# Running the first attention head by head, starting the modulation sums with the first fillers, and moving the final norm's sums into PSUM

## The chip, the cores and the metric

The kernel runs on one NeuronCore of a Trainium2 chip. TensorE (PE) multiplies matrices, VectorE (DVE), ScalarE (ACT) and GpSimd (POOL) work elementwise, and SyncE (SP) issues transfers between the device's memory and the on-chip buffers SBUF and PSUM. Each engine runs its own instructions in order; semaphores tie the engines together. The metric is the device time of one execution in microseconds (us).

## The reference

One decoder layer in float32, 512 rows of width 1024:

```
mod = silu(c) @ w_ada + b        # shift1, scale1, gate1, shift2, scale2, gate2
u   = x*(1+scale1) + shift1
q,k,v | q_down,kv_down,k_rope | g_sb,g_mla = split(u @ w_in)
A:  w[t,s] = sigmoid(z) * prod_{s<j<t}(1 - sigmoid(z_tj)),  z = q.k/8,  8 heads of width 64, s < t
B:  latent attention, softmax, 8 heads of width 96
mixed = sigmoid(g_sb)*(oA @ w_sb) + sigmoid(g_mla)*(oB @ w_mla)
x = LN1(alpha*x + gate1 * (mixed @ w_out))
u2 = x*(1+scale2) + shift2
moe: best of 4 groups, in it the best 2 of 8 experts; h = silu(u2 @ wg) * (u2 @ wu); h @ wd, weighted
x = LN2(alpha*x + gate2 * moe)
```

## The kernel before

The large projections are split products: each float32 weight becomes a rounded part `whi` (ACT, L320) and a remainder `wlo` (DVE, L321), and three matmuls per 128 rows of the contraction replace one (L330). One item of 128 output columns has 24 of them.

**Fillers.** Projection items stand in a queue `fq` (L262 to L296). `pull(n)` emits the next n steps of the queue on PE; before an item runs, its weights and those of the two items behind it are loaded and its own and the next one's are split. Loads go through the tag `raw`, a ring of two 1 MB buffers. A "mod" item is one of 16 pieces of the modulation vectors that are needed later (gate1, shift2, scale2, gate2): one 1 MB load `ra` into the same ring, and two DVE operations that add it into `macc` (L447, L449). In the kernel before the mod items stand behind the q/kv-down items (5) and the gate items (11), so they all run while the first attention runs.

**First attention** (stick-breaking, `attention_sb`, L567). For every pair of heads and every block of 128 queries it emits both heads' score matmuls (`z`, L584: head 0 in rows 0 to 63, head 1 in rows 64 to 127 of the array), both masks (L586), then the transposes `px` of the previous pair (L563), then 11.5 filler steps. Between z and px lie, per head, two sigmoids on ACT, a scan on DVE (L626) and a multiplication on POOL (L628). The second attention uses `attention` (L595): one head and block a step, with the transposes of the step before (`lag`) behind the fillers; its scores are at L773 and its masks at L774.

**Output projection.** `load_wo` (L858) loads one quarter of w_out (1 MB, `rwo`); `split_wo` (L866) multiplies the quarters of the second column half with gate1 (L875) and splits (ACT L876, DVE L877); `evac_o` (L884) multiplies by gate1, adds the residual and takes LN1's statistics. The four quarters are queued as fillers (L946), and the quarters of the second column half, (1,0) and (1,1), are loaded again later (L954, L960).

**Experts.** Twelve units of experts follow, the last two called q2 and q3 here (four experts each): gate and up products (L1352), silu times up (`sl`, ACT L1360, DVE L1361), transposes `phT` (L1367), copy `hT` (L1375), down products `py` (L1382), multiplication by gate2 (L1392), and an indirect store of the rows to the buffer `Ys` (POOL, L1398). PE, SP and POOL follow the order of the code here; DVE and ACT are ordered by the framework's cost model, except in the last unit. Ahead of the end stand: `norm_rows` (L1416), eight POOL loads of the four norm rows into `lraw`; `split_rows` (L1425), which splits them into `lrow` on DVE; `select_rows` (L1434), 26 POOL operations that build the matrices picking q3's rows for each token; `select_tr` (L1445), their transposes `pse`; `broadcast` (L1454), which spreads a norm row over 128 partitions with matmuls `pb`; and the diagonals `dg` (L1533) of the expert weights.

**Final norm** (L1646 to L1746). For each of four tiles of 128 tokens, `rs` is alpha times the LN1 output; `gts` are the two expert rows of a token, read back from `Ys`. Columns 0 to 511 (h = 0) are summed in SBUF on DVE: `base` adds the picked rows from PSUM, `add_y` adds the two expert rows (L1673). Columns 512 to 1023 (h = 1) are summed in PSUM by matmuls (L1662, L1670, L1703). Then `moments` (L1680), the scale and shift of a row (`scales`, L1686 and L1687), the normalisation on ACT (L1690), and gain and shift (L1694 and L1698) split between DVE and POOL. The overflow loop (L1602 to L1643) stands ahead of it: with these inputs its count is zero, and it is skipped.

## Time and profile before

| | us |
|---|---|
| median of 3 runs (lowest to highest) | 787.39 (787.24 to 788.0) |
| the profiled execution's own time | 790.91 |
| its span, first to last instruction | 789.2 |
| PE busy | 670.1 (85%) |
| DVE busy | 493.1 (62%) |
| mean granted TensorE clock | 0.937 |

The profiled execution is 3.5 us above the median, and its span is 1.7 us below its own time. All positions below are microseconds from the span's start. Up to 100 the projections of the first attention run, from 100 to 310 the first attention with its fillers, then the second attention, from 425 to 445 the output projection, from about 505 to 743 the experts, and from 743 on the last unit's second half and the final norm.

### The profile page before, as it was taken

The numbers are of one execution on the slowest core, as the hardware profiler recorded it, in microseconds if no ns is written. First come the engines' busy times: TensorE is split into PE (matmuls) and PEld (weight loads), VectorE is DVE, ScalarE is ACT, GpSimd is POOL, SyncE is SP. The second block draws the span as 40 slices with busy tenths as digits, with TensorE's granted clock in tenths as the row PEclk, the third lists the DMA queues.
The fourth block names the chain that finished last, engine by engine and source line by source line (L and its number), as shares of the span: only waits on it lengthen the run. The fifth ranks groups of instructions, "written<-read, shape, count | busy, mean of one in ns | idle before, by whom it ended". The sixth has DMA issues, their size and how long they took to land. (4 is left out here: it accounts for less than half of the span.)

```text
span 789.2 us, 10724 instructions
## 1 busy us (share of the span) xinstructions
PE 670.1 (85%) x3337; PEld 419.6 (53%) x3337; DVE 493.1 (62%) x1074; ACT 250.8 (32%) x545; POOL 176.5 (22%) x246
## 2 busy tenths in 40 slices
PE   5999998889989998899999873877699699972990
PEld 4778866656767775566788662433253233330230
DVE  3354379967775458977684686774725615741488
ACT  2133244533333435444341452712101110201411
POOL 2008024122233413200000013111101101136714
PEclk9999999989999999999999895989899989995996
DMA  9959763365652111361369478797999988999722
GB/s 281 344 141 336 232 220 116 114 207 180 236 179 80 44 30 34 127 184 54 107 226 365 157 279 287 254 388 252 410 407 409 382 334 314 344 405 346 307 116 106
DMA packets 83455, 184.15 MB, mean 233 GB/s; under 512 B 15442, under 2 KB 48815, under 8 KB 77499
## 3 DMA queue, kind: packets, MB, share of 16 engines
q1 hardware_dynamic: 76576, 171.70, 60.9%
q0 software_dynamic: 6736, 11.57, 4.2%
q8 instruction: 37, 0.61, 0.3%
q14 instruction: 32, 0.25, 0.1%
q10 hardware_dynamic: 74, 0.03, 0.0%
HBM read 173.30 MB, written 28.33 MB: 255 GB/s over the span
## 5 line engine op out<-in xcount | busy, mean ns | idle before, releaser
L1352 PE MATMUL pgu<-ex,xT 128*64 128x512 f32 (+1 forms) x608 | 115.0, 610 | 8.9 <-DMA ex<-in_w_exp_up_dram 5.7
L330 PE MATMUL acc<-uh,whi 128*128 128x512 f32 x224 | 91.5, 409 | 1.2 <-ACT whi L320 1.2
L330 PE MATMUL acc<-uh,wlo 128*128 128x512 f32 x224 | 89.7, 401 | 2.4 <-DVE wlo L321 2.4
L330 PE MATMUL acc<-ul,whi 128*128 128x512 f32 x224 | 89.2, 398 | 0.0
L1352 PEld LDWEIGHTS pgu<-ex,xT 128*64 128x64 f32 (+1 forms) x608 | 50.9, 129 | 66.8 <-issue 54.7
L1382 PE MATMUL py<-ex,hT 128*64 128x512 f32 (+1 forms) x304 | 63.9, 680 | 12.7 <-DVE hT L1375 8.0
L628 POOL TENSOR_TENSOR w<-be,sc 128x128 f32<-128x128 f32 (+3 forms) x32 | 41.7, 1314 | 120.2 <-DVE sc L626 62.7
L1360 ACT ACTIVATE sl<-pgu 128x256 f32<-128x256 f32 x33 | 11.5, 383 | 171.2 <-PE pgu L1352 136.7
L321 DVE TENSOR_TENSOR wlo<-raw,whi 128x1024 fp32r<-128x1024 f32 x27 | 38.8, 1445 | 21.7 <-ACT whi L320 21.7
L330 PEld LDWEIGHTS acc<-uh,wlo 128*128 128x128 f32 x224 | 42.9, 192 | 14.4 <-DVE wlo L321 3.4
L330 PEld LDWEIGHTS acc<-uh,whi 128*128 128x128 f32 x224 | 43.2, 193 | 11.7 <-ACT whi L320 1.6
L1398 POOL DMA_INDIRECT Ys<-w,msk_mla x11 | 10.9, 992 | 169.4 <-DVE w L1392 141.4
L330 PEld LDWEIGHTS acc<-ul,whi 128*128 128x128 f32 x224 | 43.0, 192 | 8.9 <-issue 0.5
L1382 PEld LDWEIGHTS py<-ex,hT 128*64 128x64 f32 (+1 forms) x304 | 16.5, 135 | 52.7 <-issue 27.7
L449 DVE SCALAR_TENSOR_TENSOR macc<-ra,rtx,macc 128x1024 f32<-128x1024 f32 x28 | 41.6, 1524 | 3.5 <-DMA ra<-in_w_ada_dram 3.4
L1361 DVE TENSOR_TENSOR sl<-pgu,sl 128x256 f32<-128x256 f32 x33 | 12.9, 418 | 41.7 <-ACT sl L1360 37.5
L626 DVE TENSOR_TENSOR_SCAN sc<-al 128x127 f32<-128x127 f32 (+3 forms) x32 | 28.7, 920 | 12.9 <-ACT al L622 12.7
L320 ACT CAST whi<-raw 128x1024 fp32r<-128x1024 f32 x27 | 28.1, 1049 | 24.7 <-PE acc L330 9.8
L563 PE MATMUL px<-ident,w 128*128 128x128 f32 x160 | 27.1, 282 | 8.4 <-POOL w L628 5.5
L1375 DVE COPY hT<-phT 128x256 f32<-128x256 f32 x33 | 13.1, 418 | 26.3 <-PE phT L1367 14.3
L1367 PE MATMUL phT<-ident,sl 128*128 128x128 f32 x32 | 8.0, 340 | 23.1 <-DVE sl L1361 20.6
L563 PEld LDWEIGHTS px<-ident,w 128*128 128x128 f32 x160 | 18.6, 143 | 16.6 <-POOL w L628 6.7
(498 smaller groups left out, 1401.2 us busy)
## 6 DMA issues: line engine op xcount, KB each, us to landing
ex<-in_w_exp_gate_dram SPq DMA_DIRECT2D x64, 512.0 KB
ex<-in_w_exp_up_dram SPq DMA_DIRECT2D x64, 512.0 KB
ex<-in_w_exp_down_dram SPq DMA_DIRECT2D x32, 1024.0 KB
ra<-in_w_ada_dram SPq DMA_DIRECT2D x16, 1024.0 KB
raw<-in_w_in_dram SPq DMA_DIRECT2D x12, 1024.0 KB
ada<-in_w_ada_dram SPq DMA_DIRECT2D x6, 1024.0 KB
rwo<-in_w_out_dram SPq DMA_DIRECT2D x6, 1024.0 KB
Ys<-dqh SPq DMA_DIRECT2D x8, 512.0 KB
```

What stands on the lines that cost most here:

```text
L320: ACT.copy(hi, w)
L321: DVE.tensor_tensor(lo, w, hi.bitcast(F32), ALU.subtract)
L330: PE.matmul(a, w_[:, k, :], part(u_, k), start=(k == 0 and n == 0), stop=(k == nk - 1 and n == 2))
L449: DVE.scalar_tensor_tensor(o, v, cact[:, k, 0:1], o, ALU.mult, ALU.add)
L563: PE.transpose(px[:, kt * P:(kt + 1) * P], w[:, kt * P:(kt + 1) * P], ident)
L626: DVE.tensor_tensor_scan(sc[:, 0:W - 1][:, ::-1], al[:, 1:W][:, ::-1], al[:, 1:W][:, ::-1], 1.0, ALU.mult, ALU.bypass)
L628: POOL.tensor_tensor(w[:, 0:W], be[:, 0:W], sc[:, 0:W], ALU.mult)
L1352: PE.matmul(ps_t[rows, :], xT[u, t][:, k, rows], ew[e, k // 4][:, :, k % 4, :], start=(k == 0), stop=(k == KD - 1))
L1360: ACT.activation(sl, ps_t[:, 0:DE], AF.Silu)
L1361: DVE.tensor_tensor(sl, ps_t[:, DE:2 * DE], sl, ALU.mult)
L1375: DVE.tensor_copy(hT[u, min(t, 1)][:, t // 2], phT[:, o:o + 256].rearrange("p (k n) -> p k n", k=2))
L1382: PE.matmul(pys[nh][rows, :], hT[u, min(t, 1)][:, t // 2, k, rows], ew[e, 2][:, k, nh * 512:(nh + 1) * 512], start=(k == 0), stop=(k == 1))
```

## The change

Five edits. (1) The mod items start behind the first filler, q3: six of them now lie ahead of the first attention, ten among the first gate items, and none behind the down items. (2) The first attention runs through `attention`, one head and block a step, 5.8125 filler steps each, lag 1. (3) A quarter of w_out that has been loaded is not loaded again: six loads of 1 MB become four. (4) The norm rows are loaded early (unit 1) by SP as 16 rows of 256 and scaled there; `select_rows` is halved over units 8 and 9; the transposes, two broadcasts and the diagonals go ahead of q2's down products, and the overflow check ahead of q3's gate and up products. (5) In the final norm the sums of h = 0 stay in PSUM, tiles 2 and 3 are scaled on POOL, and PE's and DVE's orders are rewritten.

```diff
+    def mod_item():
+        if mods_:
...
     qk3 = [(0, P, win[:, 384:512]), (P, P, win[:, 896:1024])]
     win_item("q3", "qk3", 0, qk3, lambda a: evac_q(a, 3))
+    mod_item()
     win_item("k3", "qk3", P, qk3, lambda a: ACT.copy(kT[:, 3, :], a))
+    mod_item()
...
     for i in range(4):
         win_item("v", f"v{i // 2}", (i % 2) * P, [(0, 256, win[:, C_V + (i // 2) * 256:C_V + (i // 2) * 256 + 256])], evac_v(i))
+        mod_item()
...
 
     for i, key, off, lo, n in ((3, "d3", 0, C_KVD, 256), (4, "d3", P, C_KVD, 256), (0, "d0", 0, C_QD, 256), (1, "d0", P, C_QD, 256), (2, "d2", 0, C_QD + 256, P)):
         win_item("d", key, off, [(0, n, win[:, lo:lo + n])], evac_d(i))
-        mod_item()
     for i in range(16):
         win_item("g", f"g{i // 2}", (i % 2) * P, [(0, 256, win[:, C_G + (i // 2) * 256:C_G + (i // 2) * 256 + 256])],
...
         f(wTs[h][:, 0:i + 1, i * P:(i + 1) * P], px[:, 0:(i + 1) * P].rearrange("p (k n) -> p k n", n=P))
...
-            if pend and i == NT - 1:
-                attn_out(h // 2, v, oh, ol)
...
-                zs = [pt("z", 2, "z") for b in range(2)]
-                for b in range(2):
-                    rows = slice(64 * b, 64 * b + 64)
-                    PE.matmul(zs[b][:, 0:W], qT[rows, hp, i * P:(i + 1) * P], kT[rows, hp, 0:W], start=True, stop=False)
-                for z in zs:
-                    PE.matmul(z[:, i * P:W], identb, msk_sb, start=False, stop=True)
...
@@ -616,7 +590,13 @@
         while pend:
             flush()
 
-    def weights_sb(z, W):
+    def score_sb(h, i):
+
+        W = (i + 1) * P
+        rows = slice(64 * (h % 2), 64 * (h % 2) + 64)
+        z = pt("z", 2, "z")
...
-    attention_sb(vsb, osh, osl, 11.5)
+    attention(score_sb, vsb, osh, osl, (22 * 8 + 10) / 32.0, 1)
...
@@ -857,6 +837,8 @@
 
     def load_wo(nh, kh):
         def f():
+            if ("wo", nh, kh) in raws:
+                return
             t = tmp("raw", [4, 512], F32, "rwo")
             SP.dma_start(t, w_out[0][kh * 512:(kh + 1) * 512, nh * 512:(nh + 1) * 512].rearrange("(k p) n -> p k n", p=P))
             raws["wo", nh, kh] = t
...
     fq.until("ymla")
     for nh, kh in ((0, 0), (0, 1)):
-        load_wo(nh, kh)() if ("wo", nh, kh) not in raws else None
+        load_wo(nh, kh)()
         split_wo(nh, kh)
...
-    lrow, pick = [], cp.tile([36, 4], F32R, name="pick")
+
+    lr16 = rtx[0:16, 1024:1280]
+    acol = cp.tile([16, 1], F32, name="acol")
 
     def norm_rows():
-
-        raw = tmp("wlo", [D], F32, "lraw")
-        DVE.memset(raw[0:36], 0.0)
-        for lo in (0, 32):
-            for i, v in enumerate((ln2_g, ln2_b, ln1_g, ln1_b)):
-                POOL.dma_start(raw[lo + i:lo + i + 1], v)
-        lrow.append(raw)
-
-    def split_rows():
-        raw = lrow[0]
-        lrow[0] = tmp("wlo", [D], F32R, "lrow")
-        DVE.tensor_copy(lrow[0][0:36], raw[0:36])
-        DVE.tensor_tensor(lrow[0][32:36], raw[32:36], lrow[0][32:36].bitcast(F32), ALU.subtract)
-        DVE.tensor_tensor(pick, ident[0:36, 0:4], ident[0:36, 32:36], ALU.add)
+        for i, v in enumerate((ln2_g, ln2_b, ln1_g, ln1_b)):
+            SP.dma_start(lr16[4 * i:4 * i + 4], v[0].rearrange("(c n) -> c n", c=4))
+
+    def scale_rows():
+        DVE.reduce_sum(acol, ident[0:16, 8:16], axis=AX.X)
+        DVE.tensor_scalar(acol, acol, ALPHA - 1.0, 1.0, ALU.mult, ALU.add)
+        DVE.tensor_scalar(lr16, lr16, acol, None, ALU.mult)
+
...
-    def select_rows():
+    def select_rows(a):
         u, one = units[-1], rk.rearrange("p t e -> p (t e)")
-        POOL.tensor_scalar(onesf, iot, float(u.row), None, ALU.add)
-        for a in range(u.ntl):
-            if a:
-                POOL.tensor_scalar(onesf, onesf, float(P), None, ALU.add)
+        if a < u.ntl:
+            POOL.tensor_scalar(onesf, iot if a == 0 else onesf, float(u.row if a == 0 else P), None, ALU.add)
...
+    sel_ = []
+    dg = gate1.rearrange("p (t j n) -> p t j n", t=NT, j=2)
+
     def select_tr():
+        sel_.append(tmp("wlo", [2, NT, P], F32, "sely"))
         for a in range(units[-1].ntl):
             pse = pt("z", 2, "pse")
             for t in range(NT):
                 PE.transpose(pse[:, t * P:(t + 1) * P], selw[:, a, t], ident)
-            ACT.copy(sel_y[:, a].rearrange("p t n -> p (t n)"), pse)
-    sel_y = egran[1][:, D:2 * D].rearrange("p (a t n) -> p a t n", a=2, t=NT)
...
+    def diagonals():
+        for t in range(NT):
+            for j in range(2):
+                DVE.tensor_scalar(dg[:, t, j, :], ident, w12[j][:, t:t + 1], None, ALU.mult)
+
+    def broadcast(v, dst):
         for h in range(2):
             pb = pt("z", 2, "pb")
-            PE.matmul(pb, pick[:, v:v + 1].to_broadcast([36, P]), lrow[0][0:36, h * 512:(h + 1) * 512], start=True, stop=True)
-            ACT.activation(dst[:, h * 512:(h + 1) * 512], pb, AF.Copy, scale=scale)
-
-    with tc.manual_schedule(engines=MS):
+            for q in range(2):
+                r = 4 * v + 2 * h + q
+                PE.matmul(pb[:, q * 256:(q + 1) * 256], ident[0:16, r:r + 1].to_broadcast([16, P]), lr16, start=True, stop=True)
+            ACT.copy(dst[:, h * 512:(h + 1) * 512], pb)
+
...
-            if n == len(units) - 1:
-                for t in range(NT):
-                    for j in range(2):
-                        DVE.tensor_scalar(dg[:, t, j, :], ident, w12[j][:, t:t + 1], None, ALU.mult)
-                select_tr()
             xcopy(n + 2, 0)
-            if n == len(units) - 2:
-                split_rows()
             if n > 0:
                 xcopy(n + 1, 1)
                 xcopy(n + 1, 2)
+            if n == len(units) - 2:
+                select_tr()
+                lng2[1] = tmp("whi", [D], F32, "lng2")
+                broadcast(0, lng2[0])
+                broadcast(1, lng2[1])
+                diagonals()
...
+            if n == len(units) - 2:
+                order.close()
+                overflow()
+                order.enter_context(tc.manual_schedule(engines=MS))
+                SP.dma_start(axr[0], xnd.rearrange("(t p) d -> p t d", p=P))
+                SP.dma_start(xv, xhd[256:512, :].rearrange("(t p) d -> p t d", p=P))
             if more and not pipe:
                 ps0 = pt("fil", 2, "pgu0")
+                gate_up(un, 0, ps0, range(4))
                 if n == len(units) - 2:
-                    lng2[1] = tmp("whi", [D], F32, "lng2")
-                for k in range(4):
-                    gate_up(un, 0, ps0, (k,))
-                    if n == len(units) - 2:
-                        broadcast(k, (lng2[0], lng2[1], lng1[:, 0], lng1[:, 1])[k], 1.0 if k < 2 else ALPHA)
+                    for v in range(2):
+                        broadcast(2 + v, lng1[:, v])
...
-            if n == 3 + NOV // 2:
+            if n == 1:
                 norm_rows()
-                select_rows()
+                scale_rows()
+            if 2 + NOV // 2 <= n < 4 + NOV // 2:
+                select_rows(n - 2 - NOV // 2)
...
-        scaled(DVE, 2)
...
+        for t in (2, 3):
+            scaled(POOL, t)
+
+        def add_x(t):
+            PE.matmul(sums[t, 1], ident, rs[t][:, hc[1]], start=True, stop=False)
...
-            PE.matmul(sums[t, h], sel_y[:, a, t], yb[a][:, hc[h]], start=(h == 0 and a == 0), stop=(h == 0))
-
-        def add_sel1(h, ts=range(NT)):
-            tiles(units[-1], fs[len(units) - 1], lambda a: [add_sel(t, h, a) for t in ts])
+            PE.matmul(sums[t, h], sel_[0][:, a, t], yb[a][:, hc[h]], start=(h == 0 and a == 0), stop=(h == 0))
+
+        def add_sel1(t):
+            tiles(units[-1], fs[len(units) - 1], lambda a: [add_sel(t, h, a) for h in range(2)])
+
+        def add_dg(t):
+            for j in range(2):
+                PE.matmul(sums[t, 1], dg[:, t, j, :], gts[t][:, j, hc[1]], start=False, stop=(j == 1))
+
+
+        def base(t):
+            DVE.tensor_tensor(sums[t, 0], rs[t][:, hc[0]], sums[t, 0], ALU.add)
 
...
         def add_y(t, j):
-            for h in range(2):
...
-                    DVE.scalar_tensor_tensor(o, gts[t][:, j, hc[h]], w12[j][:, t:t + 1], o, ALU.mult, ALU.add)
-
-        def src(t, h):
-            return sums[t, h] if h else rs[t][:, hc[h]]
+            DVE.scalar_tensor_tensor(sums[t, 0], gts[t][:, j, hc[0]], w12[j][:, t:t + 1], sums[t, 0], ALU.mult, ALU.add)
...
         add_x(0)
-        add_x(1)
         for t in range(NT):
             add_sel(t, 0)
-        add_sel1(0)
-
-        def base(t):
-            if t > 1:
+            if t:
                 add_x(t)
             add_sel(t, 1)
-            DVE.tensor_tensor(rs[t][:, hc[0]], rs[t][:, hc[0]], sums[t, 0], ALU.add)
-
-        for t in range(2):
-            base(t)
-            add_sel1(1, (t,))
+            add_sel1(t)
+            add_dg(t)
+        base(0)
         for t in range(NT):
-            for j in range(2):
-                add_y(t, j)
-            if t + 2 < NT:
-                base(t + 2)
-                add_sel1(1, (t + 2,))
+            add_y(t, 0)
+            if t:
+
+                scales(t - 1)
+                normed(t - 1, 0, sums[t - 1, 0])
+                dve1 = t == NT - 1
+                normed(t - 1, 1, sums[t - 1, 1] if dve1 else rs[t - 1][:, hc[1]])
+            add_y(t, 1)
+            if t + 1 < NT:
+                base(t + 1)
             moments(t)
             if t:
-                gain(DVE, t - 1, 0)
-                gain(POOL, t - 1, 1)
+                gain(DVE, t - 1, 0, sums[t - 1, 0])
+                if dve1:
+                    gain(DVE, t - 1, 1, sums[t - 1, 1])
+                else:
+                    gain(POOL, t - 1, 1, rs[t - 1][:, hc[1]])
                 for h in range(2):
                     shift(POOL, t - 1, h)
                 SP.dma_start(out[0][(t - 1) * P:t * P, :], rs[t - 1])
-            if t < NT - 1:
-                scales(t)
-                for h in range(2):
-                    normed(t, h)
...
+        for h in range(2):
+            o = rs[t][:, hc[h]]
+            DVE.scalar_tensor_tensor(o, sums[t, h], mv[:, t, 0:1], lng2[0][:, hc[h]], ALU.subtract, ALU.mult)
+            if h == 0:
+                DVE.reciprocal(mv[:, t, 2:3], mv[:, t, 2:3])
+            DVE.scalar_tensor_tensor(o, o, mv[:, t, 2:3], lng2[1][:, hc[h]], ALU.mult, ALU.add)
+            SP.dma_start(out[0][t * P:, hc[h]], o)
```

Left out here are moved definitions (`mod_item`, `load_ra`, `run_ra`) and the overflow body, which is now a function `overflow`, with other buffers and the same operations; the changed `normed` and `gain` take the source as an argument.

DVE's order at the start of the first attention; `macc` is a mod item, `wlo` the split of a filler, `sc` the scan of a head. Before:

```order
L349 COPY vsb<-pv 128x4x128
L321 TENSOR_TENSOR wlo<-raw,whi 128x1024
L447 TENSOR_SCALAR macc<-ra,rtx 128x1024 x2
L321 TENSOR_TENSOR wlo<-raw,whi 128x1024
L349 COPY vsb<-pv 128x4x128
L626 SCALAR_TENSOR_TENSOR sc<-al 128x127 x2
L449 SCALAR_TENSOR_TENSOR macc<-ra,rtx,macc 128x1024 x2
L484 TENSOR_TENSOR qdf<-acc,qdf 128x512
L321 TENSOR_TENSOR wlo<-raw,whi 128x1024
L626 SCALAR_TENSOR_TENSOR sc<-al 128x255 x2
L449 SCALAR_TENSOR_TENSOR macc<-ra,rtx,macc 128x1024 x2
```

After:

```order
L364 SCALAR_TENSOR_TENSOR macc<-ra,rtx,macc 128x1024 x2
L396 COPY vsb<-pv 128x4x128
L321 TENSOR_TENSOR wlo<-raw,whi 128x1024
L364 SCALAR_TENSOR_TENSOR macc<-ra,rtx,macc 128x1024 x2
L396 COPY vsb<-pv 128x4x128
L321 TENSOR_TENSOR wlo<-raw,whi 128x1024
L364 SCALAR_TENSOR_TENSOR macc<-ra,rtx,macc 128x1024 x2
L396 COPY vsb<-pv 128x4x128
L321 TENSOR_TENSOR wlo<-raw,whi 128x1024
L606 SCALAR_TENSOR_TENSOR sc<-al 128x127
L321 TENSOR_TENSOR wlo<-raw,whi 128x1024
L606 SCALAR_TENSOR_TENSOR sc<-al 128x255
```

Two mod operations now stand behind each of the first splits, and the first scans stand singly with splits between them.

DVE's order in the output projection, where `rwo` is the multiplication with gate1, `wo` the remainder, and `o`, `xr_B` and `stats` are `evac_o`. Before:

```order
L875 TENSOR_TENSOR rwo<-rwo,gate 128x512 x3
L877 TENSOR_TENSOR wo<-rwo,wo 128x512 x3
L875 TENSOR_TENSOR rwo<-rwo,gate 128x512 x2
L887 TENSOR_TENSOR o_3315<-o_3315,gate 128x512
L877 TENSOR_TENSOR wo<-rwo,wo 128x512
L888 SCALAR_TENSOR_TENSOR xr_B_3066<-xr_B_3066,o_3315 128x512
...
L877 TENSOR_TENSOR wo<-rwo,wo 128x512
L889 BN_STATS stats_3101<-xr_B_3067 128x6
L875 TENSOR_TENSOR rwo<-rwo,gate 128x512 x3
```

After:

```order
L857 TENSOR_TENSOR rwo<-rwo,gate 128x512 x3
L859 TENSOR_TENSOR wo<-rwo,wo 128x512 x3
L857 TENSOR_TENSOR rwo<-rwo,gate 128x512 x3
L859 TENSOR_TENSOR wo<-rwo,wo 128x512
L857 TENSOR_TENSOR rwo<-rwo,gate 128x512 x2
L869 TENSOR_TENSOR o_3315<-o_3315,gate 128x512
...
L871 BN_STATS stats_3100<-xr_B_3067 128x6
L871 BN_STATS stats_3101<-xr_B_3067 128x6
L859 TENSOR_TENSOR wo<-rwo,wo 128x512 x4
```

All eight multiplications `rwo` now stand ahead of the first `o`; before, three of them followed the eight tiles' evacuation.

DVE's order in the final norm around the statistics of tile 2 (`gt` is an expert row, `mv` the statistics and scale of a row, the last row the gain of tile 1). Before:

```order
L1686 RECIPROCAL mv<-mv 128x1
L1687 SCALAR_TENSOR_TENSOR mv<-mv 128x1
L1673 SCALAR_TENSOR_TENSOR ex_3813<-gt_7724,wt,ex_3813 128x512 x2
L1680 BN_STATS stats_3100<-ex_3813 128x6
L1680 BN_STATS stats_3100<-sums 128x6
L1681 BN_AGGR mv<-stats_3100 128x2
L1694 TENSOR_TENSOR ex_3509<-ex_3509,rtx 128x512
```

After:

```order
L1668 SCALAR_TENSOR_TENSOR sums<-gt_7713,wt,sums 128x512
L1678 RECIPROCAL mv<-mv 128x1
L1679 SCALAR_TENSOR_TENSOR mv<-mv 128x1
L1668 SCALAR_TENSOR_TENSOR sums<-gt_7713,wt,sums 128x512
L1390 UNCONDITIONAL_BRANCH
L1665 TENSOR_TENSOR sums<-ex_3809,sums 128x512
L1672 BN_STATS stats_3100<-sums 128x6 x2
L1673 BN_AGGR mv<-stats_3100 128x2
L1685 TENSOR_TENSOR ex_3505<-sums,rtx 128x512
```

The two `add_y` now write `sums` (PSUM) in place of `ex` (SBUF), and the reciprocal and the small operation behind it moved between them.

## Rows read from the trace of the kernel before

**Rows 1.** Busy time by stretch; first row names the columns.

```profile
core 0: us, PE busy (x) PEld busy (x) DVE busy (x) ACT busy (x) POOL busy (x), PEclk, DMA share, GB/s
70.00:80.00 10.00, 10.00 (x46) 8.29 (x45) 3.37 (x2) 3.21 (x5) 6.33 (x4) 1.00 1.04 377
110.00:270.00 160.00, 147.41 (x683) 104.77 (x682) 117.90 (x113) 65.40 (x121) 52.14 (x68) 0.97 0.45 149
430.00:440.00 10.00, 6.89 (x31) 4.88 (x29) 10.00 (x19) 3.76 (x5) 0.00 (x0) 0.87 0.65 262
745.00:789.00 44.00, 23.12 (x76) 7.94 (x73) 37.88 (x55) 10.17 (x16) 15.45 (x12) 0.84 0.36 140
```

**Rows 2.** PE timeline, first attention; start us, length us, operation.

```profile
126.21 1.13 PE L584 MATMUL z<-kT,qT 64*128 64x512 f32 x4
127.28 0.28 PE L586 MATMUL z<-msk_sb,identb 128*128 128x128 bf16 x2
...
130.33 0.90 PE L563 MATMUL px<-ident,w 128*128 128x128 f32 x3 [1.39 <-POOL w L628]
...
137.83 0.49 PE L584 MATMUL z<-kT,qT 64*128 64x128 f32 x4
138.25 0.28 PE L586 MATMUL z<-msk_sb,identb 128*128 128x128 bf16 x2
```

**Rows 3.** PE timeline, second attention, one head a step.

```profile
326.47 1.02 PE L773 MATMUL z<-km,qm 96*128 96x512 f32 x2
327.33 0.22 PE L774 MATMUL z<-msk_mla,identb 128*128 128x128 bf16 x1
...
329.17 0.39 PE L773 MATMUL z<-km,qm 96*128 96x128 f32 x2
329.39 0.22 PE L774 MATMUL z<-msk_mla,identb 128*128 128x128 bf16 x1
```

**Rows 4.** The page, fifth section: the mod operations on DVE.

```profile
L449 DVE SCALAR_TENSOR_TENSOR macc<-ra,rtx,macc 128x1024 f32<-128x1024 f32 x28 | 41.6, 1524 | 3.5 <-DMA ra<-in_w_ada_dram 3.4
```

**Rows 5.** DVE timeline, first multiplication of w_out with gate1.

```profile
424.25 1.89 DVE L875 TENSOR_TENSOR rwo<-rwo,gate 128x512 f32<-128x512 f32 x3 [10.83 <-DMA rwo<-in_w_out_dram]
```

**Rows 6.** PE timeline, units q2 and q3.

```profile
723.53 0.70 PE L1367 MATMUL phT<-ident,sl 128*128 128x128 f32 x2 [12.96 <-DVE sl L1361]
725.56 3.64 PE L1382 MATMUL py<-ex,hT 128*32 128x512 f32 x16 [1.33 <-DVE hT L1375]
...
732.39 1.41 PE L1352 MATMUL pgu<-ex,xT 128*32 128x512 f32 x8 [0.33 <-DMA ex<-in_w_exp_down_dram]
...
739.35 3.64 PE L1352 MATMUL pgu<-ex,xT 128*32 128x512 f32 x32
```

**Rows 7.** DVE timeline, the split of the norm rows and the diagonals.

```profile
722.43 0.71 DVE L1428 CAST lrow<-lraw 36x1024 fp32r<-36x1024 f32 x1 [17.08 <-DMA lraw<-in_ln_b_dram]
...
744.84 4.82 DVE L1533 TENSOR_SCALAR ex<-ident,wt 128x128 f32<-128x128 f32 x8
```

**Rows 8.** POOL timeline, first and last operation of select_rows.

```profile
717.57 0.55 POOL L1436 TENSOR_SCALAR onesf<-iot 128x128 f32<-128x128 f32 x1
...
736.75 0.46 POOL L1443 TENSOR_TENSOR gate<-gate,rk 128x128 f32<-128x128 f32 x1
```

**Rows 9.** DVE timeline, final norm.

```profile
758.79 1.53 DVE L1673 SCALAR_TENSOR_TENSOR ex<-gt,wt,ex 128x512 f32<-128x512 f32 x2
...
765.05 0.68 DVE L1680 BATCH_NORM_STATS2 stats<-ex 128x6 f32<-128x512 f32 x1
...
767.24 1.25 DVE L1687 SCALAR_TENSOR_TENSOR mv<-mv 128x1 f32<-128x1 f32 x1
768.41 3.50 DVE L1673 SCALAR_TENSOR_TENSOR ex<-gt,wt,ex 128x512 f32<-128x512 f32 x2
...
785.13 0.69 DVE L1698 TENSOR_TENSOR ex<-ex,lng 128x512 f32<-128x512 f32 x1
```

**Rows 10.** POOL timeline, final norm.

```profile
764.68 1.27 POOL L1694 TENSOR_TENSOR ex<-ex,rtx 128x512 f32<-128x512 f32 x1 [15.89 <-ACT ex L1690]
```

217 lines of the change are left out of this document (91 added, 126 removed).

## The prediction

> **What bounds the kernel now.** I read the busy times of stretches first. TensorE is the bound nearly everywhere (670.1 of 789.2 us busy, in the table above), so the question is where it stands still or runs at the lower clock, and who ends that. In the stretch of the first attention, 110 to 270, it is busy 147.41 of 160 us at a granted clock of 0.97, while DVE is busy 117.90 [rows 1]: 12.6 us are idle and 0.03 x 160 = 4.8 us go to the clock, 17.4 us together. From 430 to 440, in the output projection, DVE is busy for all of the 10 us and PE for 6.89 at a clock of 0.87 [rows 1]. Then the timelines of single engines. In the first attention PE stands 1.39 us in front of a transpose, waiting for POOL's product `w` [rows 2]; before that stand the scan on DVE and the sigmoids on ACT. At unit q2 PE stands 12.96 us in front of `phT` for DVE's `sl` [rows 6], and DVE had stood 17.08 us for the last of the POOL-issued norm rows, with `sl` behind the cast [rows 7]. Last comes the final norm: from 745 on DVE is busy 37.88 of 44 us [rows 1], so there DVE is the bound.
>
> **First attention and the fillers ahead of it: -0.3.** What goes: six of the sixteen mod items leave the attention, each two operations of 1.524 us [rows 4], 18.3 us in all, so DVE falls from 117.9 to about 99.6 of 160. What comes: the chain from score to transpose is one head's, where it was a pair's, behind the same cover: two times 5.8125 filler steps with lag 1, against 11.5. In the pair, the second head's scan and product stood behind the first's, and it is such a product that PE waits for. I expect half of the 17.4 us back, 8.7; none and all are the ends, since no row shows the new order.
>
> What it costs: the scores are no longer a pair. A pair takes 127.28 - 126.21 = 1.07 us from score to mask at width 512 and 138.25 - 137.83 = 0.42 at width 128 [rows 2]. A single head in the second attention takes 327.33 - 326.47 = 0.86 and 329.39 - 329.17 = 0.22 [rows 3]. Over the four widths, with the means of the end ones, a pair costs 4 x 0.745 = 2.98 and two singles 2 x 4 x 0.54 = 4.32; the difference, 1.34, times four pairs is 5.4 us on PE. The single row has 96 rows of the array and not 64, so below it I keep 0 (half of a pair per head), and above it 11.9 (a single head as long as a pair: 4 x 2.98 more).
>
> The rows say that the pair's matmuls overlap, as the pair is 1.07 and not twice 0.86. The Trainium skill, "TensorEngine Tiling (Array Packing)", section "Theoretical Speedup", gives up to a factor 2 for a contraction of 64 or less in separate halves of the array, which speaks against this edit: by that rule in full, un-pairing costs the upper end, 11.9 us, and the sum would be 6.5 us worse. The rows show 4.32 to 2.98, a factor 1.45, and I stay with them.
>
> The six mod loads of 1 MB now stand among the loads of q3, k3 and v, in a ring of two buffers that the weights share. From 70 to 80 the transfers are full (share 1.04, 377 GB/s) and PE too (10.00) [rows 1]. Six loads at that rate are 6.3 MB / 377 GB/s = 16.7 us. That is the upper end, if none of it finds a gap and each holds the next weights up; 0 is the lower. I take 3: part of what fills that row are transfers that PE doesn't wait for, and they move back. The 18.3 us of mod work lie there beside a DVE that is busy 3.37 of 10 [rows 1]. The sum is -8.7 + 5.4 + 3 = -0.3, between -17.4 and +22.
>
> **Output projection: -4.** Two of the loads of 1 MB go. DVE's first multiplication with gate1 had waited 10.83 us for such a load [rows 5]; at the 262 GB/s of that stretch two loads are 8 us. With it done earlier, all eight multiplications stand ahead of the eight evacuations. In the 10 us from 430, PE lost 3.1 us idle and 1.3 us of clock [rows 1], 4.4 us. I count 4: four remainders still stand behind the evacuations. The ends are 0 and -8. The router's chain and the expert loads behind it start earlier by the same time; if the loads of the experts did not start earlier, nothing of it would be left.
>
> **Units q2 and q3: -2.** The cast of the norm rows goes, so `sl` of q2 runs as soon as PE is through, at 723.53 - 12.96 = 710.57 [rows 6]. But now the transposes of the pick matrices, two broadcasts, and on DVE the eight diagonals stand ahead of q2's down products. The pick matrices take POOL from 717.57 to 737.21, 19.6 us [rows 8], half of it a unit earlier. The second half, 9.8 us, can begin when unit 9's rows are stored: DVE was through with them at 722.43 - 17.08 = 705.35 [rows 7]; with some 2 us for two stores, an estimate, POOL ends at 717.2. Then come eight transposes, two copies and two broadcasts of two halves with their copies on ACT, some 5 us (an estimate): q2's `py` starts at 722 in place of 725.56 [rows 6]. The diagonals, 4.82 us [rows 7], lie on a DVE without other work there. Of the gain of 3.5 I take off 1 for the overflow check on all engines ahead of q3 and 0.5 for broadcasts in full float32, neither of which a row shows alone (ends 0 and 3 together). What is late next is the weights: q3's first product waited for a transfer already [rows 6], so from 732.39 on little can come earlier unless loads do. The ends are +2 and -11 (most of the 12.96).
>
> **Final norm: -8.** From the end of q3's gate and up products, 739.35 + 3.64 = 742.99 [rows 6], to the span's end at 789.2 are 46.2 us. On DVE the diagonals (4.82 [rows 7]) and the scaling of tile 2 leave this stretch; before, the first `add_y` began at 758.79 [rows 9], 15.8 us behind 742.99, and I put the first `base` at 9 us behind it. A tile then takes `base` 0.68, two `add_y` 1.53 as when POOL is quiet, two statistics 1.36, a gain 0.69, the small operations 0.5 (an estimate) [rows 9]: 4.8, and 5.8 where the small product behind the reciprocal is held by POOL, as the one of 1.25 us is [rows 9]; 5.3 x 4 = 21.2. The last tile's four operations are 3.5, and the store behind the last one took 789.2 - 785.82 = 3.4 [rows 9]. 9 + 21.2 + 3.5 + 3.4 = 37.1, and 38 with waits for PE's matmuls between: -8.
>
> What this rests on is `add_y`. With both tensors in SBUF it takes 1.53 us for two at 758.79 and 3.50 at 768.41, while POOL works [rows 9]. Writing to PSUM it has one tensor in SBUF, as the statistics at 765.05, which stay at 0.68 [rows 9] while POOL's gain runs from 764.68 to 765.95 [rows 10]. No row has the new form beside POOL: if it is held like the old one, three tiles take 2 us more, and -2 is left; the other end is -12. The Trainium skill, "SBUF — State Buffer", section "SBUF: two separate sides", says that DVE and GpSimd lock a shared pair of ports, and that of DVE's float32 operations without a fast mode those with two SBUF inputs are held. By that rule the new `add_y` is free and the term is -8; the two rows agree with it.
>
> **Sum.** -0.3 - 4 - 2 - 8 = -14.3, so 790.91 - 14.3 = 776.6 for an execution under the profiler; the median stood 3.5 below that one, so 773.
>
> **Rivals.**
> - *Only the tail pays.* The attention keeps its stalls, because DVE's scans remain as long and the un-pairing costs 5.4 without anything recovered, and the experts are held by their transfers, so that the 4 and 2 us are lost: +5.4 + 3 - 8 - 2 = about -2 to -6, 783. For it: at 732.39 PE waited for a transfer [rows 6]. Against it: DVE loses 18.3 us in the attention. 0.18.
> - *Slower: the shared ring.* A load of weights for k3 or v has to wait until a mod load ahead of it has landed and been added, and PE, busy for 10.00 of 10 there, stands for it. Price: up to 16.7 us there, 5.4 us for the un-pairing, nothing recovered: +22, against -14 in the rest, +8: 795. It decides from 14 us of loss in the first 310 us on. For it: transfers at 1.04 from 70 to 80 [rows 1]. Against it: what fills that row is partly not for PE. 0.09.
> - *The stalls vanish.* Recovering 14 of the 17.4 us less the 5.4, 5 in the output projection, 5 at q2 and 10 at the end: -28.6, 759. For it: all of these waits hang on DVE, which is relieved. 0.2.
> - *The gain at q2 is not made* since `pse` takes the place of the norm rows as what PE waits for: the forecast without its 2, 775; it lies in the forecast's own range of 767 to 779.
>
> **How the numbers follow.** The forecast has 0.49, the rivals 0.18, 0.09 and 0.2, and 0.04 is left for gains and losses that cancel. A measurement of this kernel tells 0.2% (1.6 us) from no change. Faster is 0.49 + 0.18 + 0.2 = 0.87, same 0.04, slower 0.09. The range reaches from the good rival to beyond the tail-only one, 760 to 786, and leaves out the slower one and half of the best.
>
> **What would show it.** In the profile of the changed kernel: no idle PE from 64 to 105 (else the ring); PE busy above 147.41 in a like stretch of the attention, and waits for `w` shorter than 1.39; no wait of 10 us for `rwo` and PE above 6.89 in the 10 us where DVE is full; in front of q2's `phT` no wait, but one in front of `pse` until about 717 less what was gained before; in the final norm pairs of `add_y` at 1.5 beside POOL. An attention longer by 10 us, or `add_y` at 3.5, would make the forecast wrong.

## The result, and the profile after

The changed kernel takes 799.37 us (median of 4 runs, 795.21 to 799.99) beside 787.69 for the kernel before: a ratio of 1.0114 with a 95% interval of 1.0075 to 1.0153. The two medians are 11.7 us apart, and the ratio makes it some 9 us (6 to 12): it is slower, and the forecast was 773 with 760 to 786. Its profiled execution spans 797.8 us.

Eight marks that both traces have cut the span into stretches (start of the first q3 product; end of the last v transpose; first score and end of the last score of the second attention; end of the last product `oh` of the output projection; first product of the experts; end of q3's gate and up products; end). The columns are lengths in us, the first the mark itself; they are read from PE's timeline. (The texts on record below count the fill to the start of the last v transpose, which is 0.6 to 1.0 us less.)

| kernel | q3 at | fill | 1st attention | 2nd | to oh's end | router | experts | end | span |
|---|---|---|---|---|---|---|---|---|---|
| before | 63.8 | 36.3 | 198.6 | 39.6 | 128.6 | 24.2 | 251.9 | 46.2 | 789.2 |
| after | 61.6 | 55.2 | 202.1 | 40.6 | 121.6 | 23.9 | 254.2 | 38.6 | 797.8 |
| difference | -2.2 | +18.9 | +3.5 | +1.0 | -7.0 | -0.3 | +2.3 | -7.6 | +8.6 |

So the output projection and the final norm came about as forecast or better, the units q2 and q3 lost a little, the attention did not gain, and most of the surprise is in the fill: six projection items that took 36.3 us take 55.2. (The -2.2 ahead of it is no effect: in the fourteen traces of this document the first q3 product lies anywhere from 60.5 to 63.9.) The rows of stretches (us, PE busy, PEld, DVE, ACT, POOL, then PE's granted clock, share of the transfers, GB/s), first the fill of the kernel before, then the changed kernel, whose output projection lies some 18 us later than that of [rows 1]:

```profile
63.80:100.10 36.30, 36.30 (x172) 29.59 (x171) 13.04 (x13) 12.12 (x16) 12.18 (x8) 1.00 0.82 281
```

```profile
61.60:116.80 55.20, 45.92 (x167) 33.13 (x165) 22.85 (x21) 10.25 (x14) 17.13 (x10) 0.88 0.88 281
60.00:120.00 60.00, 49.54 (x180) 35.73 (x179) 26.93 (x27) 14.01 (x21) 18.49 (x12) 0.88 0.83 270
120.00:319.00 199.00, 193.28 (x849) 135.30 (x848) 124.96 (x135) 80.87 (x151) 54.51 (x82) 0.99 0.34 109
447.00:457.00 10.00, 10.00 (x47) 8.27 (x46) 10.00 (x17) 3.99 (x5) 0.00 (x0) 1.00 0.40 161
```

In the fill PE idles 9.3 us (10.5 from 60 to 120) and its clock is 0.88, where the kernel before had no idle time and 1.00. Afterwards the attention is nearly without idle time, and the output projection has none: in its 10 us in which DVE is full, PE is busy for 10.00 at 1.00, where [rows 1] had 6.89 at 0.87. PE's timeline at the seam of two v items, after:

```profile
84.61 0.39 PE L330 MATMUL acc<-uh,wlo 128*128 128x512 f32 x1
85.67 0.66 PE L395 MATMUL pv<-ident,vt 128*128 128x128 f32 x4 [0.68 <-ACT vt L392]
86.62 0.50 PE L330 MATMUL acc<-uh,whi 128*128 128x512 f32 x1 [0.29 <-ACT whi L320]
86.95 0.40 PE L330 MATMUL acc<-ul,whi 128*128 128x512 f32 x1
88.24 0.80 PE L330 MATMUL acc<-uh,wlo 128*128 128x512 f32 x1 [0.89 <-DVE wlo L321]
88.84 0.63 PE L330 MATMUL acc<-uh,whi 128*128 128x512 f32 x1
89.26 0.63 PE L330 MATMUL acc<-ul,whi 128*128 128x512 f32 x1
```

Between two items PE waits for the transposes' source, for the cast `whi` and for the remainder `wlo`, 1.9 us in all, and then goes at half pace (0.43 us from product to product in place of 0.23) for some 3 us: from 88.2 to 91.6 the granted clock is 0.51, the lower of its two levels, and from 91.6 to 95.0 it is 0.99. ACT's timeline tells why the cast is late. Before, then after:

```profile
80.78 1.05 ACT L320 CAST whi<-raw 128x1024 fp32r<-128x1024 f32 x1
86.20 0.59 ACT L345 COPY vt<-acc 128x512 f32<-128x512 f32 x1 [4.37 <-PE acc L330]
86.68 1.05 ACT L320 CAST whi<-raw 128x1024 fp32r<-128x1024 f32 x1
```

```profile
95.17 0.58 ACT L392 COPY vt<-acc 128x512 f32<-128x512 f32 x1 [8.60 <-PE acc L330]
95.65 1.05 ACT L320 CAST whi<-raw 128x1024 fp32r<-128x1024 f32 x1
105.33 0.58 ACT L392 COPY vt<-acc 128x512 f32<-128x512 f32 x1 [8.64 <-PE acc L330]
105.82 1.05 ACT L320 CAST whi<-raw 128x1024 fp32r<-128x1024 f32 x1
```

The two pictures look alike, `vt` (the evacuation of an item) and then a cast. But in the first the cast at 86.68 is that of the item after the next: an evacuation ends at 86.79, and PE goes on without a wait because its weights were cast at 80.78. In the second the cast at 95.65 is that of the very next item, and PE stands until it has it (86.62 and 88.24 above are such a seam, one item earlier). The queue splits a running item and the one behind it in the list. Behind each item now stands a mod item, which has no split. So the look-ahead of one item is spent on nothing, and every cast comes after the evacuation. No cast of the changed kernel waits for a transfer there: ACT's waits from 60 to 120 are for PE and, once, for POOL.

At q2 the wait for `sl` is 0.93 us where [rows 6] had 12.96, and three others stand in its place. PE's timeline after:

```profile
724.41 0.51 PE L1349 MATMUL phT<-ident,sl 128*128 128x128 f32 x2 [0.93 <-DVE sl L1343]
724.75 0.80 PE L1429 MATMUL pse<-ident,gate 128*128 128x128 f32 x5
727.42 0.48 PE L1429 MATMUL pse<-ident,gate 128*128 128x128 f32 x1 [1.88 <-POOL gate L1419]
729.51 0.47 PE L1429 MATMUL pse<-ident,gate 128*128 128x128 f32 x1 [1.61 <-POOL gate L1419]
731.59 0.48 PE L1429 MATMUL pse<-ident,gate 128*128 128x128 f32 x1 [1.61 <-POOL gate L1419]
...
732.00 7.19 PE L1442 MATMUL pb<-rtx,ident 16*128 16x256 f32 x16
739.12 3.64 PE L1364 MATMUL py<-ex,hT 128*32 128x512 f32 x16
...
746.33 3.98 PE L1334 MATMUL pgu<-ex,xT 128*32 128x512 f32 x32 [1.16 <-PEq L1448]
750.24 3.84 PE L1442 MATMUL pb<-rtx,ident 16*128 16x256 f32 x16
```

The transposes `pse` wait in three steps, 5.1 us, for POOL, whose second half of `select_rows` ends at 731.5. The experts begin 13.9 us later than before, so this is 717.6 in the time of the kernel before. Then two broadcasts take 7.2 us; the other two, the same 16 products, take 3.84 at 750.24, so those at q2 run at half pace, right behind the waits (the granted clock is 0.50 from 732.0 to 739.2 and 0.98 from 750.2 to 754.0). `py` of q2 starts at 739.12; 724.41 to 739.12 is 14.7 us where the kernel before had 2.0 after a wait of 13.0.

In the final norm `add_y` in PSUM is not held by POOL. DVE and POOL after:

```profile
781.25 0.75 DVE L1668 SCALAR_TENSOR_TENSOR sums<-gt,wt,sums 128x512 f32<-128x512 f32 x1
...
782.10 0.59 DVE L1679 SCALAR_TENSOR_TENSOR mv<-mv 128x1 f32<-128x1 f32 x1
782.62 0.74 DVE L1668 SCALAR_TENSOR_TENSOR sums<-gt,wt,sums 128x512 f32<-128x512 f32 x1
```

```profile
781.42 2.49 POOL L1689 TENSOR_TENSOR ex<-ex,lng 128x512 f32<-128x512 f32 x2 [1.68 <-DVE ex L1685]
```

While POOL works from 781.42 to 783.9, `add_y` takes 0.75 and 0.74, where two had taken 3.50 [rows 9]. The small product behind the reciprocal takes 0.59 there in place of 1.25.

### The profile page after: what moved, and what is told of

It is laid out like the page before. It is cut to its first block, busy times and chain, and to the rows that moved or that the text cites. A ratio compares the mean times of both kernels' runs of the same rounds, so it can differ in the third digit from the quotient of the medians.

```text
span 797.8 us, 10760 instructions
## 1 busy us (share of the span) xinstructions
PE 693.3 (87%) x3361; PEld 434.1 (54%) x3361; DVE 477.4 (60%) x1070; ACT 253.2 (32%) x546; POOL 171.4 (21%) x240
## 5 line engine op out<-in xcount | busy, mean ns | idle before, releaser
L330 PE MATMUL acc<-uh,whi 128*128 128x512 f32 x224 | 94.4, 421 | 3.0 <-ACT whi L320 3.0
L330 PE MATMUL acc<-uh,wlo 128*128 128x512 f32 x224 | 92.5, 413 | 4.6 <-DVE wlo L321 4.6
L330 PE MATMUL acc<-ul,whi 128*128 128x512 f32 x224 | 91.3, 408 | 0.0
L1334 PEld LDWEIGHTS pgu<-ex,xT 128*64 128x64 f32 (+1 forms) x608 | 53.1, 130 | 68.5 <-issue 63.6
L608 POOL TENSOR_TENSOR w<-be,sc 128x128 f32<-128x128 f32 (+3 forms) x32 | 36.3, 1135 | 154.2 <-DVE sc L606 139.3
L1342 ACT ACTIVATE sl<-pgu 128x256 f32<-128x256 f32 x33 | 11.5, 383 | 167.2 <-PE pgu L1334 133.1
L321 DVE TENSOR_TENSOR wlo<-raw,whi 128x1024 fp32r<-128x1024 f32 x27 | 34.9, 1295 | 27.5 <-ACT whi L320 22.6
L1343 DVE TENSOR_TENSOR sl<-pgu,sl 128x256 f32<-128x256 f32 x33 | 12.9, 418 | 51.8 <-ACT sl L1342 47.6
L364 DVE SCALAR_TENSOR_TENSOR macc<-ra,rtx,macc 128x1024 f32<-128x1024 f32 x28 | 39.7, 1448 | 6.5 <-DMA ra<-in_w_ada_dram 6.4
L1357 DVE COPY hT<-phT 128x256 f32<-128x256 f32 x33 | 13.1, 419 | 36.5 <-PEq L1390 21.1
L565 PEld LDWEIGHTS px<-ident,w 128*128 128x128 f32 x160 | 20.4, 142 | 15.0 <-issue 8.0
L567 DVE COPY wT<-px 128x256 f32<-128x256 f32 (+1 forms) x32 | 17.6, 551 | 15.4 <-PE px L565 15.0
```

Source lines behind the costliest of these rows:

```text
L321: DVE.tensor_tensor(lo, w, hi.bitcast(F32), ALU.subtract)
L330: PE.matmul(a, w_[:, k, :], part(u_, k), start=(k == 0 and n == 0), stop=(k == nk - 1 and n == 2))
L364: DVE.scalar_tensor_tensor(o, v, cact[:, k, 0:1], o, ALU.mult, ALU.add)
L565: PE.transpose(px[:, kt * P:(kt + 1) * P], w[:, kt * P:(kt + 1) * P], ident)
L567: f(wTs[h][:, 0:i + 1, i * P:(i + 1) * P], px[:, 0:(i + 1) * P].rearrange("p (k n) -> p k n", n=P))
L608: POOL.tensor_tensor(w[:, 0:W], be[:, 0:W], sc[:, 0:W], ALU.mult)
```

## Experiments

The medians of one kernel scatter by some 4 us from run to run, and its single executions by up to 11 (one of a_late_pairs, of 3665 us, is not counted). Each trace is of one execution, but the lengths of an untouched stretch scatter less: the stretch to `oh`'s end is 121.5 or 121.6 in every kernel that has edit 3 and the end 38.6 in every one that has edit 5, while the second attention varies by 2.1 (39.5 to 41.6) and the experts of the same code by 1 to 2. So edits are judged by their stretch, and the whole by the ratio.

| kernel | fill | 1st attention | experts | span | ratio to before (95%) |
|---|---|---|---|---|---|
| a_lookahead | 48.6 | 199.1 | 254.1 | 788.1 | 1.0041 (1.0004 to 1.0078) |
| b_empty | 54.8 | 204.9 | 250.1 | 812.1 | 1.0316 (1.0256 to 1.0376) |
| a_mods_late | 36.4 | 203.2 | 253.2 | 778.6 | 0.9925 (0.9887 to 0.9962) |
| a_late_pairs | 36.4 | 198.4 | 253.2 | 774.3 | 0.9894 (0.9854 to 0.9934) |
| a_ring2 | 52.2 | 198.9 | 253.3 | 792.1 | 1.0065 (1.0027 to 1.0104) |
| a_la_ring2 | 43.3 | 196.8 | 254.0 | 779.2 | 0.9942 (0.9909 to 0.9975) |
| p_z_apart | 36.8 | 203.3 | 253.5 | 781.9 | 0.9898 (0.983 to 0.9967) |
| p_select_early | 36.4 | 198.5 | 248.1 | 771.7 | 0.9785 (0.971 to 0.986) |
| p_best | 35.9 | 201.6 | 247.2 | 773.7 | 0.9841 (0.9793 to 0.9889) |
| a_best | 43.7 | 196.8 | 248.6 | 774.2 | 0.9842 (0.9797 to 0.9888) |
| a_best_sin | 36.5 | 196.8 | 248.5 | 766.5 | 0.976 (0.972 to 0.9801) |
| best_pairs | 36.4 | 195.3 | 247.7 | 766.8 | 0.9723 (0.9682 to 0.9763) |

**Look-ahead or ring.** Theory 1: a mod item takes the look-ahead's place. Theory 2: weights and mod loads share two buffers, and transfers are full.

b_empty, the kernel before with empty items:

```diff
+    fq.add("nop", lambda: None, lambda: 0, lambda w: iter(()))   # behind q3, k3 and each v
```

> The kernel before, with six empty items in the queue behind q3, k3 and the four v items: no load, no split, no operation, no step. Theory 1 (an item without a split takes the look-ahead's place): the order of ACT becomes that of the changed kernel, the v items take about 9 to 10 us each, and the median rises from 787.5 to about 803 (798 to 808). Theory 2 (ring and transfers): nothing is loaded, so the time stays at 787 to 789.

The fill went from 36.3 to 54.8, without one load or operation more; PE's waits there are those of the changed kernel, as a table of waits from 60 to 120 shows (what waits and for whom: us, times, longest). First the changed kernel, then b_empty:

```profile
PE acc L330 <- DVE wlo L321: 4.6, 6, 0.9
PE acc L330 <- ACT whi L320: 3.0, 6, 1.6
PE pv L395 <- ACT vt L392: 2.8, 4, 0.7
```

```profile
PE acc L330 <- DVE wlo L321: 5.6, 6, 1.5
PE acc L330 <- ACT whi L320: 3.8, 6, 1.6
PE pv L350 <- ACT vt L347: 2.8, 4, 0.7
```

ACT's waits in that time are all for PE, none for a transfer. The lost look-ahead is by itself enough for the whole 18.5 us. (The median, 814.15, went beyond the forecast 798 to 808: the kernel lost 6.3 us in the attention too, and that stays open.)

a_lookahead, the changed kernel:

```diff
-            for n in range(i, min(i + ns, len(self.items))):
+            j = i + 1
+            while j < len(self.items) and self.items[j].name == "mod":
+                j += 1
+            for n in (i, j):                  # the running item and the next one with a split
...
```

> The changed kernel, with one edit in the filler queue: the split ahead of a running item skips mod items, so that the next projection's cast (ACT) and remainder (DVE) are again issued one item ahead. Loads, ring and mod operations stay where they are. Theory 1 (the mod item, which has no split, takes the look-ahead's place, so the cast of the next weights stands behind the evacuation of the item before): the items k3 to the last v go back from 10.1 us each to about 5.5, TensorE idles under 2 us from 60 to 120 instead of 10.5, and the median falls from 799 to about 780 (776 to 785). Theory 2 (the ring of two buffers that weights and mod loads share, and full transfers): the loads come no earlier, the items stay near 10 us each, and the median stays at 795 to 800.

Only 6.6 of the 18.9 us came back, and the median, 791.32, met neither forecast. PE's waits changed their owner, and behind PE ACT's casts now wait for the weights themselves. PE's row, then ACT's, from 60 to 120:

```profile
PE acc L338 <- ACT whi L328: 8.4, 3, 4.6
```

```profile
ACT whi L328 <- DMA raw<-in_w_in_dram: 20.8, 3, 10.1
```

So something of theory 2 lies underneath: once the look-ahead is mended, the weights come late. The next two runs tell whether the ring or full transfers hold them up.

a_la_ring2 and a_ring2 give the first six mod loads buffers of their own, with and without the mended look-ahead:

```diff
-            t = tmp("raw", [4, 512], F32, "ra")
+            t = gran(("R4", "R5")[k % 2], [4, 512], F32, "ra") if half == 0 and k < 6 else tmp("raw", [4, 512], F32, "ra")
```

> The changed kernel with the look-ahead that skips mod items and, besides, the first six mod loads in two buffers of their own (memory of a later stage) in place of the ring that the weights use. With the look-ahead alone the stretch from the first q3 product to the last v transpose was 47.6 us (changed kernel 54.6, kernel before 35.7), and the casts waited for the weights' transfers. Theory A (what is left is the shared ring): the stretch falls to 36 to 39 us and the median to some 9 us below that kernel's 791, 782. Theory B (what is left are full transfers, six loads of 1 MB more in that time): the stretch stays at 45 to 48 us and the median at 789 to 792.

> The changed kernel with the two buffers of their own for the first six mod loads, and the look-ahead as it is (a mod item takes its place). If the two causes are each enough by itself, the lost look-ahead still costs all of its time: the stretch stays near 54 us, as with six empty items (54.1), and the median near 799. If the ring were the main cause it would fall below 45 us.

With the look-ahead mended, own buffers bring the fill from 48.6 to 43.3, between the two forecasts, and the casts no longer wait for the weights: the ring was the second limit. Alone they leave 52.2 (median 794.39), and what they bring there is not a wait less: PE idles 9.3 us in the fill as in the changed kernel, and the 3.0 us lie in the clock, 0.93 in place of 0.88:

```profile
63.20:115.40 52.20, 42.91 (x167) 30.80 (x165) 23.49 (x19) 10.24 (x14) 17.12 (x10) 0.93 0.81 278
```

Neither mend alone does it, both together give 11.9 of the 18.9 us. The 7 us that were left had one place. ACT's and PE's timelines of a_la_ring2:

```profile
71.67 0.59 ACT L394 COPY kT<-acc 128x512 f32<-128x512 f32 x1 [3.91 <-PE acc L338]
78.97 0.72 ACT L547 ACTIVATE rtx<-ang,rc 128x512 f32<-128x512 f32 x1 [6.71 <-POOL ang L470]
79.60 1.03 ACT L328 CAST whi<-raw 128x1024 fp32r<-128x1024 f32 x1
```

```profile
80.68 0.80 PE L338 MATMUL acc<-uh,whi 128*128 128x512 f32 x1 [3.61 <-ACT whi L328]
```

The cast at 79.60 stood behind the sine of the rotary table, which waited 6.71 us for POOL's angles. (POOL's eleven operations for them took 21.2 us here and 16.8 in the kernel before; what slowed them beside the mod operations was not tested.) a_best_sin issues the sine behind the first v item (see below), and the fill is 36.5: early mod items then cost nothing there.

a_mods_late undoes edit 1 alone (mod items again behind the down items, 6.0 steps a block). a_late_pairs undoes edit 2 as well (`attention_sb` with 11.5 steps).

> The changed kernel with edit 1 undone: no mod item among q3, k3 and v, five behind the down items and eleven among the gate items, as in the kernel before; steps per block of the first attention raised from 5.8125 to 6.0 for the six more items. Both theories expect the fill stretch as in the kernel before (its first v item at 75, the last at 98) and some of the attention's waits back: about 783 (778 to 788). If edit 1 were not the cause it would stay at 797 to 800.

> The changed kernel with edits 1 and 2 undone: mod items at their old places and both heads of a pair in one step with 11.5 filler steps. Left of the change are edits 3 to 5. From the traces: output projection -7, units q2 and q3 +2, final norm -8, so about 775 (771 to 779) if nothing else moves. Against the kernel with only edit 1 undone it gives the price of edit 2: by the prediction's 5.4 us for un-pairing it is some 5 us below that one if the waits of the pairs are small, and equal or above if one head at a time gives back as much as it costs.

Both fills are 36.4. Edit 1 was worth 799.37 - 784.19 = 15 us of the loss by the medians, as by the ratios, and 19.2 by the two spans. Edit 2 lengthened the attention from 198.4 to 203.2; by the medians, 782.23 and 784.19, it cost 2.0. (With 782.23 a_late_pairs missed its 771 to 779. Its traced execution took 775.97, close to its lowest, 775.82.)

**Un-pairing.** p_z_apart is a_late_pairs with each head's mask right behind its scores:

```diff
-                for z in zs:
-                    PE.matmul(z[:, i * P:W], identb, msk_sb, start=False, stop=True)
+                    PE.matmul(zs[b][:, i * P:W], identb, msk_sb, start=False, stop=True)
```

> Edits 3 to 5 of the change with the paired attention of the kernel before (782 us), in which each head's mask now stands right behind its scores, so that the two heads' score matmuls are no longer neighbours; chain, order and filler steps of the pair stay. It measures un-pairing by itself. If the price of un-pairing is the lost overlap of the two heads' matmuls, the time from a pair's first score to its last mask rises as the prediction's 1.34 us per pair of heads over four widths, and the attention by about 5 us (787). If the 4.8 us that one head a step costs have another cause (the shorter cover, the order of fillers), it stays at 781 to 783.

The attention rose by 4.9 us to 203.3, just as with one head a step; the medians of the two kernels (782.2 and 782.3) show nothing of such a step. So the 4.8 or 4.9 us rest on traced executions: 198.4 to 198.6 with pairs and late mod items (three kernels), 203.2 and 203.3 without pairs (two). A single head's scores in the changed kernel take as long as a pair's in [rows 2] (1.05 and 0.41 from score to mask, against 1.07 and 0.42), which by the prediction's own sum makes 4 x (2 x 4 x 0.73 - 2.98) = 11.4 us of more work:

```profile
133.09 1.12 PE L598 MATMUL z<-kT,qT 64*128 64x512 f32 x2
134.14 0.23 PE L599 MATMUL z<-msk_sb,identb 128*128 128x128 bf16 x1
...
140.33 0.48 PE L598 MATMUL z<-kT,qT 64*128 64x128 f32 x2
140.74 0.23 PE L599 MATMUL z<-msk_sb,identb 128*128 128x128 bf16 x1
```

PE's busy time in the attention, with pairs and with the scores apart (columns as in the stretches above):

```profile
98.00:297.00 199.00, 184.67 (x854) 131.68 (x853) 141.25 (x147) 81.60 (x154) 59.54 (x80) 0.97 0.43 138
```

```profile
100.00:304.00 204.00, 194.45 (x855) 135.26 (x853) 141.11 (x147) 82.32 (x154) 59.62 (x80) 0.97 0.42 134
```

PE is busy for 9.8 us more, of which 4.9 lengthen the stretch; the rest fills what was idle time.

**Units q2 and q3.** p_select_early is a_late_pairs with the two halves of `select_rows` three units earlier:

```diff
-            if 2 + NOV // 2 <= n < 4 + NOV // 2:
-                select_rows(n - 2 - NOV // 2)
+            if 5 <= n < 7:
+                select_rows(n - 5)
```

> Edits 3 to 5 of the change (782 us) with the two halves of select_rows on GpSimd behind units 5 and 6 in place of 8 and 9. In the changed kernel TensorE waited 5.1 us in three steps for them ahead of q2's down products, and then took 7.2 us for two broadcasts. If that wait is on the path, the end of q3's gate and up products comes 4 to 5 us earlier and the median is 778; if the transfers of q2's and q3's weights set the time, only the wait moves (to a DMA) and the median stays at 781 to 783.

The experts' stretch fell from 253.2 to 248.1, and the transposes no longer wait. Its PE timeline:

```profile
704.70 0.51 PE L1369 MATMUL phT<-ident,sl 128*128 128x128 f32 x2 [0.93 <-DVE sl L1363]
705.04 1.04 PE L1449 MATMUL pse<-ident,gate 128*128 128x128 f32 x8
...
712.78 3.64 PE L1384 MATMUL py<-ex,hT 128*32 128x512 f32 x16
...
720.20 3.98 PE L1354 MATMUL pgu<-ex,xT 128*32 128x512 f32 x32 [1.32 <-PEq L1468]
```

From `phT` to `py` are now 8.1 us in place of 14.7, and the weights were there. Edit 4 as written cost 1.3 to 2.3 us, with this mend it saves 3 to 5 (against the 251.9 of the kernel before; the same code took 250.1 in b_empty).

**All together.** p_best is p_select_early with the mended look-ahead; a_best is the whole change with the three mends; a_best_sin adds the sine; best_pairs is that with the pairs.

```diff
         fq.until("k3")
+        fq.pull(12)
         ACT.activation(rtab, ang, AF.Sin, scale=rc[:, 2:3])
```

> Edits 3 to 5 with the paired attention and the mod items at their old places, select_rows behind units 5 and 6, and the look-ahead that skips mod items. If an item without a split also cost time inside the attention, where every down item and eleven gate items have a mod item behind them, the stretch from the last v transpose to the second attention falls from 198.5 us to about 192 (with one head a step it fell from 203.2 to 196.8), and the median from 773 to about 767. If the attention's own cover hides the late casts, nothing changes there: 198 and 773.

> The whole change (early mod items, one head a step) with its three defects mended: look-ahead that skips mod items, own buffers for the first six mod loads, select_rows behind units 5 and 6. From the stretches of the kernels measured: fill 43.3, attention 196.8, then 121.6 to the end of the output projection, 248 for the experts, 38.5 for the end; 779.2 less 6 is 773 for the span, 778 for the median. Against the kernel with pairs and late mod items it should be 5 to 10 us slower, if early mod items cost transfers in the fill stretch and un-pairing costs 4.8 us; if the relief of VectorE in the attention were worth more than that, it would be equal or faster.

> The whole change with the look-ahead that skips mod items, own buffers for the first six mod loads, select_rows behind units 5 and 6, and now the sine of the rotary table on ScalarE (it waits for GpSimd's angles) issued behind the first v item and not ahead of its cast. Without this last edit the fill stretch was 43.3 to 43.7 us, and the only long wait in it was 3.6 us of TensorE for a cast that stood behind the sine, then half-clock products. If the sine is what is left, the stretch falls to 37 and the median from 776 to about 770; if it is the transfers, it stays at 42 to 44 and 776.

> The same kernel with the paired attention of the kernel before. If un-pairing costs 4.8 us in any case, the attention falls from 196.8 to 192 and the median to about 765; if one head a step is what lets the look-ahead pay (with pairs and late mod items it did not: 201.6 against 198.5), the attention stays at 196 to 200.

p_best is a miss: with pairs and late mod items the look-ahead bought nothing (201.6 us, 198.5 without). a_best missed as well: it is equal to p_best and not slower. With the sine moved the mended change is at 0.976 of the kernel before, best_pairs at 0.9723. The two overlap; the pair is worth 1.5 us of the attention there and not 4.8, so best_pairs' 195.3 met neither of its two forecasts. But p_select_early, without edits 1 and 2, is at 0.9785 (0.971 to 0.986), which overlaps with both (the spans are 771.7, and 766.5 and 766.8): what is shown to pay are edits 3 to 5 with `select_rows` moved, and the mends take the loss out of edits 1 and 2 without a gain of theirs being shown.

## Why the prediction was wrong

The sum was -14.3, and the span grew by 8.6: 22.9 us apart, 15.9 of them in the fill and 6.8 in the attention. By its own steps:

- **First attention and the fillers ahead of it: -0.3 forecast, +20.2 measured** (-2.2 + 18.9 + 3.5). Here it failed, at the term "I take 3" for the six mod loads: the fill lost 18.9 us. The term weighed transfers and buffers alone, and it came out beyond its own upper end of 16.7, for a reason that it did not contain. What an item takes from the queue besides its load, the place in the look-ahead, was not asked, though the rule of the queue stood in the description of the kernel. b_empty shows that this is enough for all of it. The ring, the mechanism of the slower rival, was a second limit, which shows only once the look-ahead is mended (own buffers then bring 5.3 us), and the sine a third (7.2).
- **Half of the 17.4 us back: not so.** The attention of the changed kernel is 3.5 us longer. If un-pairing costs 4.9 there, as with late mod items, 1.4 came back and not 8.7. DVE's busy time in the stretch fell by 13.4 us (140.9 to 127.4) and not by 18.3. With the seams mended the attention is 196.8; with un-pairing at 4.9 that is 6.7 back, with the 1.5 of best_pairs it is 3.3.
- **Un-pairing, 5.4: the size came out by luck, the reason was wrong.** I took a single head's price from the second attention, 0.86 us [rows 3], and it is 1.05. The work that it adds is then near the upper end of 11.9: 11.4 us by the rows of single heads, 9.8 by PE's busy time. Half of that was hidden in waits, which is why the attention grew by 4.9. The Trainium skill, "TensorEngine Tiling (Array Packing)", section "Theoretical Speedup", gives up to a factor 2 for a contraction of 64; the trace agrees with the page (two singles of 1.05 against a pair of 1.07, a factor 1.96), against the row that I preferred to it, which was of 96 rows and of another loop.
- **Output projection: -4 forecast, -7.0 measured**, inside its ends; all eight multiplications ahead of the evacuations, and no wait of PE from there to `oh`'s end, where it had stood 1.96 us for a remainder.
- **Units q2 and q3: -2 forecast, +2.3 measured**, just past its end of +2. POOL ended at 717.6 in the time of the kernel before, and 717.2 was forecast. What was mis-sized are the broadcasts: from POOL's end to `py` I had 5 us, and it is 7.6 (731.5 to 739.12), so `py` came 0.3 us earlier and not 3.5; and in q3's gate and up products, where I had 0.5 for them, the stretch from its first product to its end grew from 10.6 to 12.9.
- **Final norm: -8 forecast, -7.6 measured**, by the step that was given: `add_y` in PSUM at 0.75 beside POOL.
- **Of the rivals**, the slower one gave 795 by "the shared ring", with 0.09. It came nearest to the 799, but by luck: the sign given for it, idle PE from 64 to 105, came, and no cast waited for a transfer there; its mechanism is the lesser part. The 0.87 for faster rested on the attention being neutral.

Not settled: why empty items also lengthen the attention by 6.3 us, why the look-ahead lengthens it with pairs and late mod items by 3.1, and why un-pairing costs 4.9 us of it with late mod items and 1.5 with the early ones and the mends.

## What to carry to other kernels

Before a step is put into a queue that looks ahead by a count of items, ask what it takes from the others: a step with nothing to prepare uses up the preparation of the one behind it, and an empty one costs as much as a full one. When a cause is found by undoing an edit, mend it and see whether the time comes back: here three limits lay on top of each other (look-ahead, ring, sine), and each hid the next. Take the price of an operation from a row of the same shape, or keep the whole range.
